# Summing the squares of the first norm on TensorE instead of on VectorE and GpSimd, in a two-layer encoder kernel

## The chip, the cores and the metric

One core of one Trainium2 chip runs the whole program. The metric is the device time of one execution in microseconds (us), the median of three runs. The engines are PE (TensorE: matmuls; PEld is its weight load), DVE (VectorE), ACT (ScalarE), POOL (GpSimd) and SP (SyncE, which issues the DMAs). Each engine works through its own queue in order.

## The reference

Two encoder layers over 512 tokens of 1024 features, float32. The change touches the start of layer 0, the first RMS norm:

```python
def rms(x, g):
    xf = x.astype(F32)
    y = xf * lax.rsqrt(jnp.mean(xf * xf, axis=-1, keepdims=True) + EPS)
    return (y * g.astype(F32)).astype(x.dtype)

    for layer in range(DEPTH):
        h = rms(x, g_mix[layer])
        (aq, ..., dv, gate) = jnp.split(h @ w_in[layer], split_points, axis=-1)
        o_a, o_b, o_c, o_d = ...                   # four attention branches
        br = jnp.einsum('bsmc,mcd->bsmd', o, w_branch[layer])
        g = jax.nn.sigmoid(gate.reshape(b, s, N_BRANCH, D_MODEL))
        x = x + jnp.einsum('bsmd,bsmd->bsd', g, br) @ w_out[layer]
        ...                                        # cross-attention, then the MLP
```

## The kernel before, in words

x lies transposed: 128 features on the partitions, the 512 tokens along the free axis, so 8 tiles `X` of 128x512 (`KD` = 8). Every large product is three fp32r matmuls (`mm3`, L177 to L179): high part by high part, high by low, low by high. So each weight tile is loaded (`wload`), cast to its high part `whi` by ACT (L299), and the low part `wlo` is subtracted by POOL in four pieces (L167 as called there). A norm's gain is multiplied into x ahead of the product (tiles `s`), and the per-token factor 1/rms (`r_mix`) is applied to the products, because it is known only later.

The start of layer 0 is `Norm.add_first`, once for each of the 8 tiles of x: it writes the scaled high part (ACT L348 or DVE L346) and low part (DVE L349), and ACT squares x (L355). The squares of even tiles are added up in the buffer `of` by DVE, those of odd tiles in the buffer `z` by POOL (L357). `Norm.finish` then sums both over the partitions: for each block of 128 tokens (`NTB` = 4) two fp32 matmuls with one column, the partial sum as weights and a column of ones as data (L364). DVE makes the mean (L367), POOL takes the power -1/2 (L368), DVE copies it to `r_mix` (L370). With `want_row=True` the same numbers are also wanted along the free axis: DVE spreads them on a diagonal (L374, which needs the identity matrix `idr`, loaded by DMA and cast at L234), PE multiplies that by ones (L377), and DVE copies the row to `Rrow` (L379).

Around it stand: `front_B0`, the first projection, four token blocks of 24 matmuls of 128x416 (banks `dn`, `dn`, `sc`, `sc`), each block read by ACT with `r_mix` (L412, L413), then reduced (L415), scaled (L669 to L675) and transposed by PE (L679); `layer_tables` (L269 to L289), small tables that DVE makes from one DMA each; `front_B` for pairs of heads (power on POOL at L716 to L718, scaling on DVE at L722 to L727); and `gate_piece`, which fills PE's time:

```python
        ps = psum("df")
        for k in range(KD):
            t = norm.xg[k]
            i = mm3(ps, gh[:, k, :], gl[:, k, :], t[:, 0, :], t[:, 1, :], k == 0, k == KD - 1)
            chain("fill", *i)
        z = tl("zg", [P, S])
        V.tensor_tensor(out=z, in0=ps, in1=norm.R, op=ALU.mult)
```

A gate piece is 24 matmuls of 128x512 into the bank `df`, of which there is one. Its reader is the multiplication with `Rrow` on DVE, L785, and the next gate piece can't start until it has run. `PB = dict(dn=2, sc=2, tr=2, pv=1, df=1)` gives the number of PSUM banks per name; of the SBUF buffers `of` and `z` there is one each, of `p` five.

What order an engine's instructions have is not written out: the tile scheduler of the framework merges the program's parts into a queue for each engine by its own estimates, and waits are on semaphores. An edit in one place can so shift rows on all engines.

Of the kernel before, what the change touches and what calls it, by code (L numbers as in the profile page):

```python
# [13 lines left out]
ALU = mybir.AluOpType  # L14
AX = mybir.AxisListType

P = 128
S = 512
D = 1024
KD = D // P  # L20
# [3 lines left out]
NTB = S // P  # L24
# [69 lines left out]
def kernel(  # L94
# [18 lines left out]
    V, A, G, T, SY = nc.vector, nc.scalar, nc.gpsimd, nc.tensor, nc.sync  # L113
# [12 lines left out]
    def tl(tag, shape, dt=F32):  # L126
        cnt[0] += 1
        return sp.tile(shape, dt, tag=tag, name=f"{tag}{cnt[0]}", bufs=BUFS[tag])

    def slot(dt=F32R, tag="s"):  # L130
        return tl(tag, [P, 2, S], dt)
# [4 lines left out]
    def ptile():  # L136
        return tl("p", [P, S + 2])

    def ztile():
        return tl("z", [P, S])  # L140

    def stat(n):
        return tl("st", [P, 8])[:, :n]
# [4 lines left out]
    def psum(tag, dt=F32):  # L148
        cnt[0] += 1
        return pp.tile([P, S], dt, tag=tag, name=f"{tag}{cnt[0]}", bufs=PB[tag])  # L150

    def const(name, shape, dt=F32):
        return cp.tile(shape, dt, tag=name, name=name)

    def f(ap):
        return ap.bitcast(F32)

    def bc(ap, axis, n):
        a = ap.unsqueeze(axis)
        shp = list(a.shape)  # L160
        shp[axis] = n
        return a.to_broadcast(shp)
# [28 lines left out]
    def big():  # L191

        rot["big"] += 1
        return ("dn", "dn", "df")[(rot["big"] - 1) % 3]
# [7 lines left out]
    ones = const("ones", [P, P])  # L202
# [21 lines left out]
    def fcol(l, name, i):  # L224
        o, _ = FEAT_OFF[name]
        return ftile[:, l, o + i:o + i + 1]
# [87 lines left out]
    class Norm:  # L314


        def __init__(self, l, gname):
            self.l, self.g = l, gname
            self.xg = [None] * KD
            self.ss = None  # L320
            self.r = self.R = self.R2 = None

        def add(self, m, x, c0=0):
# [17 lines left out]
        def add_first(self, m, x):  # L341

            g = fcol(self.l, self.g, m)
            t = self.xg[m] = slot()
            if m % 2:
                V.tensor_scalar(t[:, 0, :], x, g, None, op0=ALU.mult)  # L346
            else:
                A.activation(t[:, 0, :], x, AF.Copy, scale=g)  # L348
            V.scalar_tensor_tensor(out=t[:, 1, :], in0=x, scalar=g, in1=f(t[:, 0, :]), op0=ALU.mult, op1=ALU.subtract)  # L349
            if m < 2:  # L350
                q = tl("of", [P, S]) if m == 0 else tl("z", [P, S])
                self.ss = (self.ss or []) + [q]
            else:
                q = ptile()[:, :S]
            A.activation(q, x, AF.Square)  # L355
            if m >= 2:
                (G if m % 2 else V).tensor_tensor(out=self.ss[m % 2], in0=self.ss[m % 2], in1=q, op=ALU.add)  # L357

        def finish(self, want_row=False):
            ps = psum("tr")  # L360
            parts = self.ss if isinstance(self.ss, list) else [self.ss]
            for tb in range(NTB):
                for i, s in enumerate(parts):
                    T.matmul(ps[:, tb:tb + 1], lhsT=s[:, tb * P:(tb + 1) * P], rhs=ones[:, 0:1], start=i == 0,  # L364
                             stop=i == len(parts) - 1)
            r = stat(NTB)
            V.tensor_scalar(r, ps[:, :NTB], 1.0 / D, EPS, op0=ALU.mult, op1=ALU.add)  # L367
            G.tensor_tensor(out=r, in0=r, in1=mhalf[:, :NTB], op=ALU.pow)  # L368
            keep = rkeep[self.g]
            V.tensor_copy(keep, r)  # L370
            self.r = keep
            if want_row:
                dg = ztile()
                V.tensor_tensor(out=dg.rearrange("p (t c) -> p t c", t=NTB), in0=bc(idf, 1, NTB),  # L374
                                in1=bc(keep, 2, P), op=ALU.mult)
                pr = psum("tr")
                T.matmul(pr, lhsT=ones, rhs=dg, start=True, stop=True)  # L377
                self.R = Rrow
                V.tensor_copy(Rrow, pr)  # L379
# [624 lines left out]
    for l in range(L):  # L1004
# [39 lines left out]
        for spec in FILL.split("_"):  # L1044
            parts = []
# [9 lines left out]
        for i, (b, j) in enumerate(units):  # L1055
# [3 lines left out]
            parts = fill[i] if len(fill[i]) > 1 else [[]] + fill[i]  # L1059
# [35 lines left out]
        for i in range(4):  # L1095
            cs = slice(i * P, (i + 1) * P)
            ps = psum(big())
# [182 lines left out]
```

## Time and profile before

| what | value |
|---|---|
| runs | 2365.25, 2367.22, 2368.31 us; median 2367.22 |
| profiled execution | 2368.6 us, span of the profile 2366.8 us |
| busy share of the span | PE 97%, PEld 83%, DVE 59%, POOL 55%, ACT 49% |
| L357 (the additions) | 3 on DVE, 3 on POOL |
| granted TensorE clock | 0.993 of full speed on the mean |

Busy time alone says little here, since PE is busy nearly always: what counts is where PE waits, and who it waits for. The views used are the table of waits of one engine, the timeline (start, duration, engine, line, operation, out<-in, number of like instructions; in brackets the idle time ahead of it and what ended it), the summary of a source line, and the table of stretches. The distance from one start to the next is the time an instruction takes in a full queue, since neighbours overlap.

### The profile page before, as it was taken

The page shows a single profiled execution, that of the slowest core. Times are in us where ns is not written, and L with a number is a line of the kernel's source. Part 1 is how long each engine was busy: PE and PEld are TensorE (multiplying, and loading weights), DVE is VectorE, ACT ScalarE, POOL GpSimd, SP SyncE. Part 2 cuts the span into 40 slices and gives each one's busy share as a digit, 9 for nine tenths or more (in the row PEclk, how much of TensorE's full clock was granted, in tenths as well). Part 3 has the DMA queues.
Part 4 walks back from the last instruction along what each step waited for, and adds up shares of the span by engine and source line. Part 5 has one row for each costly group of instructions (what it writes and reads, how often), then busy time and mean ns, then how long its engine had stood idle before and what let it go on. Part 6 is the DMA issues. An engine that isn't in the chain of part 4 may idle for free.

```text
span 2366.8 us, 33717 instructions
## 1 busy us (share of the span) xinstructions
PE 2287.4 (97%) x12032; PEld 1962.2 (83%) x12032; DVE 1395.9 (59%) x2996; ACT 1153.7 (49%) x2269; POOL 1300.4 (55%) x1657
## 2 busy tenths in 40 slices
PE   7999999999999999999999999999999999999999
PEld 6788889887877788888888888898888778888887
DVE  7777676788964742222457676768888648222222
ACT  4555656655653642223345565566556446322321
POOL 7554454625365576666665535455452654766663
PEclk9999999999999999999999999999999999999999
DMA  5332242352454233333342213424425532323332
GB/s 174 96 98 68 84 142 79 122 162 73 152 184 144 76 98 96 91 98 98 106 134 92 87 56 106 133 79 154 128 88 169 168 109 84 107 91 97 98 95 84
DMA packets 90953, 260.36 MB, mean 110 GB/s; under 512 B 9832, under 2 KB 14568, under 8 KB 90784
## 3 DMA queue, kind: packets, MB, share of 16 engines
q1 hardware_dynamic: 90784, 258.20, 34.6%
q8 instruction: 95, 1.56, 0.3%
q14 instruction: 74, 0.61, 0.1%
HBM read 224.56 MB, written 33.60 MB: 109 GB/s over the span
## 4 chain that ended last, share of the span: by engine, by line
PE 72%; DVE 11%; POOL 5%; DMA 4%; issue 4%; ACT 3%; SPq 0%; POOLq 0%; ACTq 0%; DVEq 0%
PE dn L177 11%; PE dn L178 11%; PE dn L179 11%; PE df L177 8%; PE df L179 8%; PE df L178 8%; POOL wlo L167 4%; DMA wst<-in_wts_dram 3%; PE tr L476 2%; DVE pt L480 1%; ACT whi L299 1%; PE dn L403 1%; PE sc L177 1%; PE sc L179 1%; PE sc L178 1%
## 5 line engine op out<-in xcount | busy, mean ns | idle before, releaser
L167 POOL TENSOR_TENSOR wlo<-wst,whi 128x256 fp32r<-128x256 f32 (+3 forms) x1400 | 1073.9, 799 | 797.4 <-ACT whi L299 719.9
L299 ACT CAST whi<-wst 128x1024 fp32r<-128x1024 f32 (+3 forms) x350 | 349.8, 1002 | 660.1 <-PE dn L178 287.5
L177 PE MATMUL df<-s,whi 128*128 128x512 f32 (+1 forms) x967 | 383.7, 397 | 18.0 <-DVE zg L785 9.9
L179 PE MATMUL df<-s,wlo 128*128 128x512 f32 (+1 forms) x967 | 377.9, 391 | 0.0
L178 PE MATMUL df<-s,whi 128*128 128x512 f32 (+1 forms) x967 | 377.0, 390 | 0.0
L177 PE MATMUL dn<-whi,s 128*128 128x384 f32 (+4 forms) x736 | 248.2, 343 | 11.7 <-ACT s L348 7.6
L178 PE MATMUL dn<-wlo,s 128*128 128x384 f32 (+4 forms) x736 | 249.2, 341 | 1.1 <-POOL wlo L167 1.0
L179 PE MATMUL dn<-whi,s 128*128 128x384 f32 (+4 forms) x736 | 249.4, 340 | 0.0
L177 PEld LDWEIGHTS df<-s,whi 128*128 128x128 f32 x967 | 183.0, 189 | 56.8 <-DVE zg L785 13.7
L179 PEld LDWEIGHTS df<-s,wlo 128*128 128x128 f32 x967 | 183.1, 189 | 37.4 <-POOL wlo L167 0.7
L178 PEld LDWEIGHTS df<-s,whi 128*128 128x128 f32 x967 | 183.3, 190 | 33.2 <-issue 0.2
L177 PE MATMUL dn<-s,whi 128*128 128x512 f32 (+1 forms) x529 | 197.9, 377 | 3.1 <-ACT s L599 1.2
L178 PE MATMUL dn<-s,whi 128*128 128x512 f32 (+1 forms) x529 | 198.7, 377 | 0.4 <-DVE s L167 0.4
L179 PE MATMUL dn<-s,wlo 128*128 128x512 f32 (+1 forms) x529 | 198.0, 375 | 0.1
L177 PEld LDWEIGHTS dn<-whi,s 128*128 128x128 f32 x736 | 139.6, 191 | 21.0 <-ACT s L348 7.6
L479 ACT CAST pt<-tr 128x512 fp32r<-128x512 f32 (+1 forms) x224 | 123.0, 557 | 68.2 <-PE tr L476 66.7
L480 DVE TENSOR_TENSOR pt<-tr,pt 128x512 fp32r<-128x512 f32 (+1 forms) x224 | 142.7, 643 | 19.4 <-ACT pt L479 9.1
L178 PEld LDWEIGHTS dn<-wlo,s 128*128 128x128 f32 x736 | 140.0, 190 | 10.5 <-POOL wlo L167 3.8
L179 PEld LDWEIGHTS dn<-whi,s 128*128 128x128 f32 x736 | 139.8, 190 | 5.3
L311 POOL TENSOR_SCALAR sf<-sf 128x8 f32<-128x8 f32 (+2 forms) x44 | 13.5, 306 | 192.3 <-DVE sf L415 190.6
L177 PEld LDWEIGHTS dn<-s,whi 128*128 128x128 f32 x529 | 99.8, 190 | 21.8 <-ACT s L599 1.3
L178 PEld LDWEIGHTS dn<-s,whi 128*128 128x128 f32 x529 | 100.5, 190 | 19.0 <-DVE s L167 0.9
(392 smaller groups left out, 4895.4 us busy)
## 6 DMA issues: line engine op xcount, KB each, us to landing
wst<-in_wts_dram SPq DMA_DIRECT2D x272, 512.0 KB, 3.6
wst<-in_wts_dram SPq DMA_DIRECT2D x64, 384.0 KB, 3.0
yl<-yz SPq DMA_DIRECT2D x48, 512.0 KB, 3.6
yz<-zg SPq DMA_DIRECT2D x64, 256.0 KB, 2.1
yz<-yl SPq DMA_DIRECT2D x48, 256.0 KB, 3.0
bias<-tscr SPq DMA_DIRECT2D x16, 320.0 KB, 3.6
yl<-yz SPq DMA_DIRECT2D x16, 256.0 KB, 3.1
bias<-tscr SPq DMA_DIRECT2D x8, 448.0 KB, 3.7
```

The costliest lines, as they stand in the source:

```text
L167: (eng or V).tensor_tensor(out=dst, in0=src, in1=f(hi), op=ALU.subtract)
L177: a = T.matmul(ps, lhsT=lh, rhs=rh, start=first, stop=False)
L178: T.matmul(ps, lhsT=lh, rhs=rl, start=False, stop=False)
L179: b = T.matmul(ps, lhsT=ll, rhs=rh, start=False, stop=last)
L299: chain("wh", A.copy(hi[:, :n], st[:, :n]))
L311: G.tensor_scalar(dst, src, add, None, op0=ALU.add)
L403: T.transpose(ps[:rows_, i * P:(i + 1) * P], s, idn)
L476: T.transpose(ps[:, kb * P:(kb + 1) * P], src[:, kb * P:(kb + 1) * P], idn)
L479: A.copy(hi, pv)
L480: V.tensor_tensor(out=lo, in0=pv, in1=f(hi), op=ALU.subtract)
```

## The change

Each square goes into a buffer `p`, and right after it PE adds it to the sum: four matmuls of one column (one for each block of 128 tokens), accumulated over the 8 tiles in one bank `tr`. The additions are gone, and `finish` finds the sum ready. Later norms still use the sum in `of` (one matmul for each block, as before). Lines from L365 on have a number lower by one after the change; the new matmul is L356.

```diff
             else:
                 A.activation(t[:, 0, :], x, AF.Copy, scale=g)
             V.scalar_tensor_tensor(out=t[:, 1, :], in0=x, scalar=g, in1=f(t[:, 0, :]), op0=ALU.mult, op1=ALU.subtract)
-            if m < 2:
-                q = tl("of", [P, S]) if m == 0 else tl("z", [P, S])
-                self.ss = (self.ss or []) + [q]
-            else:
-                q = ptile()[:, :S]
+            if m == 0:
+                self.ps = psum("tr")
+            q = ptile()[:, :S]
             A.activation(q, x, AF.Square)
-            if m >= 2:
-                (G if m % 2 else V).tensor_tensor(out=self.ss[m % 2], in0=self.ss[m % 2], in1=q, op=ALU.add)
+
+            for tb in range(NTB):
+                T.matmul(self.ps[:, tb:tb + 1], lhsT=q[:, tb * P:(tb + 1) * P], rhs=ones[:, 0:1], start=m == 0 and tb == 0,
+                         stop=m == KD - 1 and tb == NTB - 1)
 
         def finish(self, want_row=False):
-            ps = psum("tr")
-            parts = self.ss if isinstance(self.ss, list) else [self.ss]
-            for tb in range(NTB):
-                for i, s in enumerate(parts):
-                    T.matmul(ps[:, tb:tb + 1], lhsT=s[:, tb * P:(tb + 1) * P], rhs=ones[:, 0:1], start=i == 0,
-                             stop=i == len(parts) - 1)
+            ps = self.ps
+            if ps is None:
+                ps = psum("tr")
+                for tb in range(NTB):
+                    T.matmul(ps[:, tb:tb + 1], lhsT=self.ss[:, tb * P:(tb + 1) * P], rhs=ones[:, 0:1], start=True, stop=True)
```

The queues change in the mixer of layer 0 (PE to about row 3250 of 10786, DVE to about row 550 of 2832) and are the same behind it. Three places show how.

**PE, first projection.** Names: `dn_283`/`dn_301`, `sc_347`/`sc_365` are banks of the projection before/after, `df_251` is the first gate piece, `tr_203`/`tr_152` the bank of the sum, `tr_218`/`tr_236` that of the row. Before, the last seven rows of the sum stood behind 76 matmuls of the projection and the gate piece, and the matmul of the row had only five matmuls of the projection behind it:

```order
L178 MATMUL sc_347<-wlo_142,s_183 128x416
L364 MATMUL tr_203<-ones,z_157 128x1
L364 MATMUL tr_203<-ones,of_152 128x1
...
L179 MATMUL df_251<-s_149,wlo_245 128x512
...
L177 MATMUL sc_379<-whi_141,s_183 128x416
L377 MATMUL tr_218<-z_216,ones 128x512
L178 MATMUL sc_379<-wlo_142,s_183 128x416
```

After:

```order
L179 MATMUL dn_333<-whi_108,s_149 128x416
L356 MATMUL tr_152<-ones,p_180 128x1 x4
L356 MATMUL tr_152<-ones,p_189 128x1 x4
L356 MATMUL tr_152<-ones,p_198 128x1 x4
L356 MATMUL tr_152<-ones,p_207 128x1 x4
L356 MATMUL tr_152<-ones,p_216 128x1 x4
L178 MATMUL dn_301<-wlo_120,s_168 128x416
...
L178 MATMUL dn_333<-wlo_120,s_177 128x416
L376 MATMUL tr_236<-z_234,ones 128x512
L179 MATMUL dn_333<-whi_119,s_177 128x416
```

Now 39 matmuls of the projection and all 32 of the sum stand ahead of the row's, and 57 of the projection behind it; the first gate piece has left the projection and follows it.

**DVE, from the tables to the row.** `st_212`/`st_230` is the mean, `z_216`/`z_234` the diagonal. Before:

```order
L280 TENSOR_TENSOR p_231<-bias_222 128x128
L367 TENSOR_SCALAR st_212<-tr_203 128x4
L282 TENSOR_REDUCE st_233<-p_231 128x2
L370 COPY r_mix<-st_212 128x4
L234 CAST idr<-z_195 128x128
L284 TENSOR_TENSOR nlam<-st_233 128x1
L285 TENSOR_SCALAR nlam<-nlam 128x1
L415 TENSOR_REDUCE sf_309<-dn_283 128x1 x3
L234 CAST jr<-z_198 128x128
...
L374 TENSOR_TENSOR z_216<-idr,r_mix 128x512
```

After:

```order
L280 TENSOR_TENSOR p_249<-bias_240 128x128
L234 CAST jr<-z_225 128x128
L366 TENSOR_SCALAR st_230<-tr_152 128x4
L282 TENSOR_REDUCE st_251<-p_249 128x2
L369 COPY r_mix<-st_230 128x4
L373 TENSOR_TENSOR z_234<-idr,r_mix 128x512
```

Both casts of identities now stand ahead of the mean (that of `idr` further up), and the diagonal follows `r_mix` at once. The tables still stand ahead of the mean.

**DVE, two gate pieces later.** `df_995`/`df_1013` is the same gate piece before and after, `tok_551`/`tok_569` the same pair of heads, `sf_552`/`sf_570` its factors. Before:

```order
L415 TENSOR_REDUCE sf_552<-dn_559 128x2
L167 TENSOR_TENSOR spl_589<-tok_517,spl_589 128x4x32
L785 TENSOR_TENSOR zg_1020<-df_995,Rrow 128x512
L174 COPY T_505<-dn_605 96x2x256
L722 TENSOR_TENSOR tok_551<-tok_551,sf_552 128x2x256
```

After:

```order
L174 COPY T_523<-dn_623 96x2x256
L721 TENSOR_TENSOR tok_569<-tok_569,sf_570 128x2x256
L722 TENSOR_TENSOR tok_569<-tok_569,sf_570 128x2x64
L174 COPY T_524<-dn_635 96x2x256
L724 TENSOR_TENSOR tok_569<-tok_569,gbn 128x2x64 x2
L726 TENSOR_TENSOR tok_569<-tok_569,gqr 128x64 x2
L167 TENSOR_TENSOR spl_655<-tok_569,spl_655 128x4x64
L784 TENSOR_TENSOR zg_1038<-df_1013,Rrow 128x512
```

The reader of the `df` bank has moved from ahead of the scaling of the heads to behind it. On POOL the four subtractions of one weight tile (128x160 each) now stand between the small power's first two steps and the power itself (L715, L716 and L717 after).

## Rows read from the trace of the kernel before

**Rows 1.** The page, parts 1 and 5: busy time and share of the span by engine, and one of the costliest groups (busy time, mean ns of one | idle time ahead of it).

```profile
PE 2287.4 (97%) x12032; PEld 1962.2 (83%) x12032; DVE 1395.9 (59%) x2996; ACT 1153.7 (49%) x2269; POOL 1300.4 (55%) x1657
...
L480 DVE TENSOR_TENSOR pt<-tr,pt 128x512 fp32r<-128x512 f32 (+1 forms) x224 | 142.7, 643 | 19.4 <-ACT pt L479 9.1
```

**Rows 2.** Waits of PE in the first 45 us: what it waited for, us in total, times, longest.

```profile
PE dn L177 <- ACT s L348: 7.6, 1, 7.6
PE df L177 <- ACT whi L299: 2.2, 1, 2.2
PE dn L679 <- DVE tok L673: 1.6, 1, 1.6
PE tr L364 <- DVE of L357: 0.7, 1, 0.7
```

**Rows 3.** Timeline of DVE, from the last table to the diagonal.

```profile
28.04 0.28 DVE L280 TENSOR_TENSOR p<-bias 128x128 f32<-128x128 f32 x1
28.24 0.15 DVE L367 TENSOR_SCALAR st<-tr 128x4 f32<-128x4 f32 x1
...
29.52 0.17 DVE L370 COPY r_mix<-st 128x4 f32<-128x4 f32 x1 [0.88 <-POOL st L368]
31.90 0.23 DVE L234 CAST idr<-z 128x128 fp32r<-128x128 f32 x1 [2.21 <-DMA z<-in_ident_dram]
...
34.25 0.68 DVE L374 TENSOR_TENSOR z<-idr,r_mix 128x512 f32<-128x512 f32 x1
```

**Rows 4.** Timeline of PE, the end of the sum before (each one-column matmul is two records): the first pair of seven in a row, and the matmul that follows them.

```profile
25.76 0.28 PE L364 MATMUL tr<-ones,z 128*128 128x1 f32 x2
...
27.24 0.48 PE L179 MATMUL df<-s,wlo 128*128 128x512 f32 x1
```

**Rows 5.** Line L357, the additions: durations in ns (least, median, longest), first and last start in us.

```profile
L357 DVE TENSOR_TENSOR of<-of,p x3: 1123/1124/1784, 10.1 to 18.6; 128x512 f32<-128x512 f32 x3
L357 POOL TENSOR_TENSOR z<-z,p x3: 1293/1723/1749, 13.5 to 23.8; 128x512 f32<-128x512 f32 x3
```

**Rows 6.** Timeline of PE at its start: two neighbours at the first pace, two at the later one.

```profile
11.28 0.55 PE L179 MATMUL dn<-whi,s 128*128 128x416 f32 x1
11.62 0.55 PE L177 MATMUL dn<-whi,s 128*128 128x416 f32 x1
...
13.10 0.35 PE L178 MATMUL dn<-wlo,s 128*128 128x416 f32 x1
13.29 0.35 PE L179 MATMUL dn<-whi,s 128*128 128x416 f32 x1
```

**Rows 7.** Timeline of PE, from the row's matmul to the second gate piece.

```profile
35.55 1.02 PE L377 MATMUL tr<-z,ones 128*128 128x512 f32 x2
36.01 0.75 PE L178 MATMUL sc<-wlo,s 128*128 128x416 f32 x1
...
42.18 0.47 PE L177 MATMUL df<-s,whi 128*128 128x512 f32 x1 [2.22 <-ACT whi L299]
42.49 0.40 PE L178 MATMUL df<-s,whi 128*128 128x512 f32 x1
42.72 0.40 PE L179 MATMUL df<-s,wlo 128*128 128x512 f32 x1
```

**Rows 8.** Timeline of DVE from 71 to 79 us: the reader of a gate piece and the scaling of a pair of heads.

```profile
71.66 0.68 DVE L785 TENSOR_TENSOR zg<-df,Rrow 128x512 f32<-128x512 f32 x1
72.26 0.68 DVE L174 CAST T<-dn 96x512 fp32r<-96x512 f32 x1
74.57 1.22 DVE L722 TENSOR_TENSOR tok<-tok,sf 128x512 f32<-128x512 f32 x1 [1.64 <-POOL sf L718]
...
77.95 0.47 DVE L727 TENSOR_TENSOR tok<-tok,gqr 128x64 f32<-128x64 f32 x2
```

**Rows 9.** Timeline of PE: waits at the start of gate pieces and around them, in layer 0.

```profile
72.40 0.50 PE L177 MATMUL df<-s,whi 128*128 128x512 f32 x1
...
79.85 0.67 PE L403 MATMUL dn<-idr,spl 128*96 128x128 f32 x4 [1.11 <-ACT spl L732]
80.72 0.54 PE L177 MATMUL df<-s,whi 128*128 128x512 f32 x1 [0.20 <-DVE zg L785]
...
169.52 0.49 PE L177 MATMUL df<-s,whi 128*128 128x512 f32 x1 [1.17 <-DVE zg L785]
...
257.84 0.50 PE L177 MATMUL df<-s,whi 128*128 128x512 f32 x1 [0.97 <-DVE zg L785]
...
280.62 0.63 PE L476 MATMUL tr<-idr,p 128*128 128x128 f32 x4 [1.26 <-DVE p L505]
```

**Rows 10.** Timeline of POOL at the same place: two of four subtractions of 128x160, then the steps of the power for a pair of heads.

```profile
68.94 1.20 POOL L167 TENSOR_TENSOR wlo<-wst,whi 128x160 fp32r<-128x160 f32 x2
71.50 0.35 POOL L716 TENSOR_SCALAR sf<-sf 128x8 f32<-128x8 f32 x1 [1.36 <-DVE sf L415]
...
72.24 2.30 POOL L718 TENSOR_TENSOR sf<-sf,mhalf 128x12 f32<-128x12 f32 x1
```

**Rows 11.** Table of stretches: us, busy time and instructions of PE, PEld, DVE, ACT, POOL, then the granted clock of PE (1.00 is full), the DMA share and GB/s.

```profile
42.20:47.00 4.80, 4.80 (x14) 3.81 (x15) 4.61 (x17) 2.17 (x8) 3.65 (x5) 0.64 0.77 183
81.00:84.50 3.50, 3.50 (x10) 2.68 (x10) 0.53 (x2) 0.59 (x2) 3.05 (x4) 0.51 0.23 80
169.50:284.00 114.50, 111.93 (x669) 100.53 (x670) 83.08 (x196) 67.60 (x150) 46.40 (x67) 1.00 0.25 80
```

More of the change, by code (lines that the diff above doesn't have):

```diff
@@ L319, in __init__ @@
             self.xg = [None] * KD
-            self.ss = None
+            self.ss = self.ps = None
             self.r = self.R = self.R2 = None
```

## The prediction

> **What bounds the kernel now.** I began with the busy shares: PE works 97% of the span, DVE, the next, 59% [rows 1]. So the time is PE's own work, plus PE's waits, plus what PE does at half clock. An engine other than PE counts only where PE waits for it. The second view is therefore PE's waits in the first 45 us, where the sum of squares is made: 7.6 us until x is there, 0.7 us for an addition of L357, 1.6 us for a product of L673, 2.2 us for the weights of the second gate piece [rows 2]. Only the 0.7 us is named after the code that goes. The third view is the way from the sum to the row: the mean runs on DVE at 28.24, but right behind the last table, L280 at 28.04 [rows 3], though the matmuls of the sum had ended by 27.24 [rows 4]. It stood in DVE's queue, not in wait for PE. That is what the edit can move: DVE's queue in front of the mean is shortened by three additions.
>
> The order of all queues changes with it, up to a third of PE's rows. So I went through both orders and gave every row its duration from the trace; the terms below are the places where PE's wait comes out different by over 1 us.
>
> **Removed.** Three additions on DVE, 1.12 + 1.78 + 1.12 = 4.02 us, and three on POOL, 1.75 + 1.72 + 1.29 = 4.76 us [rows 5]. Neither is on PE; what they free is worked out in the next part but one.
>
> **Added on PE.** 32 one-column matmuls in place of 8, so 24 more. Seven in a row took 25.76 to 27.24, 0.211 us each [rows 4], about as much as a matmul of 416 columns (0.19 at the later pace [rows 6]). Together 24 x 0.211 = 5.1 us; at the first pace (0.34 against 0.19 for the same 416 columns [rows 6]) it would be up to 9. The bounds are 0, if PE would stand there anyway, and +5.1 to +9 if not. I take 0, for this reason: ahead of the row's matmul the new order has 39 matmuls of the projection and the 32. 39 x 0.19 + 32 x 0.211 = 14.2 us, and some 15 of them at the first pace add 15 x 0.15 = 2.3. From 7.6 us [rows 2] PE is through by 24.1 at the latest (the squares are made before it, and the first eight of the new matmuls stand ahead of everything, so they run while PE waited before). The row's data comes later, as follows.
>
> **The row is earlier for DVE, and PE stands in front of it.** DVE's mean: 28.24 - 4.02 + two casts of 0.23 that moved ahead of it (L234 [rows 3]) = 24.7. From mean to the end of `r_mix` 29.52 + 0.17 - 28.24 = 1.45, then the diagonal at once, 0.68 [rows 3]: 26.8. PE, ready at 24.1 or before, waits 2.7 us or more for a diagonal that before was ready while PE was still in the projection. Behind it stand: the row's matmul 0.46 (35.55 to 36.01 [rows 7]), 57 of the projection x 0.19 = 10.7, the first gate piece 24 x 0.23 = 5.5 (42.49 to 42.72 [rows 7]), and two groups of transposes, some 0.7 each. 26.8 + 0.5 + 10.7 + 5.5 + 1.4 = 44.9 for the start of the second gate piece, which was at 42.18 [rows 7]: **+2.7 us**. The old waits of 1.6 and 2.2 us are inside this: they are gone, and cover nothing. The identity's DMA, which came late before (DVE waited 2.21 us [rows 3]), no longer needs the buffer `z` of the sum and is issued early; I cost it at nothing, and if it were late again the row would wait for it, not the mean.
>
> **The bank `df`, two pieces later.** Before, the reader of the bank ran at 71.66, ahead of the scaling of the heads, and PE's next piece started at 72.40 almost without a wait [rows 8, 9]. Now it stands behind the scaling, which needs POOL's power, and on POOL four subtractions of 0.6 (half of the 1.20 for two [rows 10]) have moved in front of that power. POOL: 71.50 to 72.24 = 0.74, + 2.4, + 2.30 [rows 10] = 5.4. DVE from there: 74.57 to 78.42 = 3.85 for the scaling, 0.6 for the copy to `T`, about 0.3 for the split, 0.68 for the reader itself [rows 8]: 5.4. Together 10.8 us after POOL begins. In the meantime PE has one gate piece (5.5) and 16 transposes (0.6 each eight), 6.9 at most with gaps. So PE waits about 3.7 us. Against it stand the waits of 1.11 and 0.20 that follow in the trace [rows 9], which this covers only in part: **+3.5 us** with the small waits before it.
>
> **Two more readers of `df` moved behind other work.** Of the gate piece `df_1493` in the new order (the third after the one above) the reader now stands behind work for attention and for a further pair of heads. From the moment when PE ends the piece that is one evacuation (0.64, the mean of L480 [rows 1]), a reduction of as many columns, taken as the same, four small rows that I estimate at 1.0 together from the 0.47 for two of L727 [rows 8], and the reader's own 0.68: 3.0 us, against eight transposes on PE, 0.9 to 1.1 us: **+1.9**. For the piece at 257.84, which waits 0.97 already [rows 9], the scaling again comes first and POOL's power starts later, behind two subtractions of 0.6: I put that wait at 3.2, so **+2.2**.
>
> **Given back.** PE comes 6 to 8 us later into the rest of layer 0 while DVE's queue there is as long as before, so waits for DVE shrink: 1.17 at 169.52 to some 0.5, 1.26 at 280.62 to some 0.4 [rows 9], and a few of 0.3 to 0.5; **-2.8** in all.
>
> Sum: 2.7 + 3.5 + 1.9 + 2.2 - 2.8 = **+7.5 us**. The profiled execution took 2368.6 (span 2366.8), so 2376.1; it lies 1.4 above the median of the runs, 2367.2, and the same sum on the median gives **2374.7**. The terms have errors of 1 to 2 us each, mostly where a queue's order decides; from these alone I give 2371.5 to 2378.
>
> [...]
>
> **Rivals.**
> 1. *No change that can be measured* (within 0.2%, 4.7 us, about what a measurement of this kernel can tell from no change). The front goes as above, but the `df` readers don't decide: DVE's wait for POOL's power is shorter, because POOL has 4.76 us less to do and its subtractions run earlier, and PE, late by 2.7, finds the bank free. Then 2.7, half of the 7.6 of the three places, and -2.8 are about +3.7: 2370.9. For it: POOL is busy 55% [rows 1]; against it: the power itself is 2.30 us and now stands behind the subtractions.
> 2. *Faster.* The row's diagonal is there when PE comes: DVE's tables run through earlier, and PE never stands. Then the waits of 0.7, 1.6 and 2.2 go, 5.1 of new work comes, and the first eight of the new matmuls lie in PE's first wait (8 x 0.34 = 2.7 at the first pace): the second gate piece starts at 42.18 - 4.5 + 5.1 - 2.7 = 40.1, so -2.1, and if the `df` readers also keep up, with the -2.8 given back, -4.9: 2362.3. It decides at the mean: it would have to run before about 21 instead of 24.7, but the tables, whose last runs at 28.04 before [rows 3], still stand in front. Little speaks for it.
> 3. *More than forecast.* Each new wait of over 2.5 us (at the row, at the two `df` pieces) is followed by a stretch at half clock, as in the trace behind 1.6 + 2.2 [rows 11]: three of 1.7, less the one that goes: +3.4 on the forecast, 2378.1. [...]
>
> **How the numbers follow.** Forecast 0.60, rival 1 0.18, rival 2 0.05, rival 3 0.17. The forecast's own lower end reaches into the band of no change with about 0.02. So faster 0.05, same 0.20, slower 0.75. The range takes the forecast, nearly all of rival 3 (to 2380.5) and the upper half of rival 1: 2369 to 2380.5.
>
> **What would show it.** Right: the L356 matmuls end before 24, PE waits 2 us or more at L376, whose diagonal ends near 26.8; the second gate piece starts near 45; the piece that was at 72.40 starts near 79 after a wait of 3 to 4 us for L784; from 400 us on everything is later by a constant 6 to 9 us. Wrong: if PE waits for L356's squares or the first projection runs longer at half clock (then the 5.1 is on the path); if the gate pieces start without waits for L784 (rival 1); if L376 doesn't wait (rival 2); if the clock is low in stretches behind the new waits (rival 3).

## The result and the profile after

The change makes the kernel slower: 2382.39 us in the median of 6 runs (2376.46 to 2390.01) against 2366.65 for the kernel before on the same chip, a ratio of 1.0072 with a 95% interval of 1.0057 to 1.0087, or +17 us (13 to 21; the medians lie 15.7 apart). A second measurement beside other kernels gave 1.0070 (1.0057 to 1.0084). The forecast was +7.5, with 2380.5 as its upper end: the sign was right, the size was not.

The profiled execution is the longest of the six (2390.0, span 2388.2), so some of its numbers are above the median's; a second trace, of the same kernel in another run (e5, span 2375.3, the shortest of its six), stands beside it where that matters.

The page's busy times, against [rows 1]: PE has 20 us more, as has its weight load; DVE and POOL have 9.1 and 4.4 less, ACT 2.0 more.

```profile
PE 2307.4 (97%) x12080; PEld 1981.7 (83%) x12080; DVE 1386.8 (58%) x2993; ACT 1155.7 (48%) x2269; POOL 1296.0 (54%) x1654
```

**The front.** The waits of PE in the first 60 us, which answer to [rows 2]:

```profile
PE tr L356 <- ACT p L353: 5.5, 2, 4.5
PE df L177 <- DVE kr_raw L586: 1.8, 1, 1.8
```

The waits of 0.7, 1.6 and 2.2 us are gone, and PE starts at 4.5 instead of 7.6, as expected. A wait of 1.8 at the second gate piece is new: the first gate piece now runs right ahead of it, and L784, the reader of their bank, starts on DVE only at 50.50. But there is no wait at L376, where the forecast had 2.7 us or more. PE's timeline shows why; these rows answer to [rows 4, 6, 7]:

```profile
4.52 1.86 PE L356 MATMUL tr<-ones,p 128*128 128x1 f32 x8 [4.52 <-ACT p L353]
7.41 1.87 PE L356 MATMUL tr<-ones,p 128*128 128x1 f32 x8 [1.03 <-ACT p L353]
...
12.06 1.70 PE L356 MATMUL tr<-ones,p 128*128 128x1 f32 x8
...
15.85 8.53 PE L356 MATMUL tr<-ones,p 128*128 128x1 f32 x40
...
27.50 0.55 PE L178 MATMUL dn<-wlo,s 128*128 128x416 f32 x1
27.85 0.55 PE L179 MATMUL dn<-whi,s 128*128 128x416 f32 x1
...
29.02 0.36 PE L178 MATMUL dn<-wlo,s 128*128 128x416 f32 x1
29.22 0.35 PE L179 MATMUL dn<-whi,s 128*128 128x416 f32 x1
...
30.92 1.02 PE L376 MATMUL tr<-z,ones 128*128 128x512 f32 x2
...
51.33 0.47 PE L177 MATMUL df<-s,whi 128*128 128x512 f32 x1 [1.75 <-DVE kr_raw L586]
```

Twenty one-column matmuls in a row (40 records) took 15.85 to 24.23, 0.42 us each, twice the 0.211 of [rows 4]. The 416-column matmuls start 0.35 apart until 28.2 and 0.19 apart behind that. So PE runs at the lower of the two paces until 28.2; before the change the same pace ended at 12.8 ([rows 6] stand on both sides of it). The row's matmul starts at 30.92 because PE gets to it then: its diagonal was ready at 26.6, which the rows of DVE show (they answer to [rows 3]):

```profile
20.94 0.28 DVE L280 TENSOR_TENSOR p<-bias 128x128 f32<-128x128 f32 x1
...
24.41 0.16 DVE L366 TENSOR_SCALAR st<-tr 128x4 f32<-128x4 f32 x1 [3.05 <-PE tr L356]
...
25.69 0.17 DVE L369 COPY r_mix<-st 128x4 f32<-128x4 f32 x1 [0.93 <-POOL st L367]
25.90 0.69 DVE L373 TENSOR_TENSOR z<-idr,r_mix 128x512 f32<-128x512 f32 x1
```

The forecast's 24.7 for the mean and 26.8 for the diagonal came out, at 24.41 and 26.59, but not for its reason: DVE was through with the tables and the cast by 21.4 and then waited 3.05 us for the sum.

**The gate pieces.** Their waits, from PE's timeline (answering to [rows 9]; the pieces that started at 72.40, 103.69 and 257.84 before):

```profile
84.45 0.50 PE L177 MATMUL df<-s,whi 128*128 128x512 f32 x1 [1.39 <-DVE zg L784]
...
122.36 0.50 PE L177 MATMUL df<-s,whi 128*128 128x512 f32 x1 [2.31 <-DVE zg L784]
...
269.84 0.50 PE L177 MATMUL df<-s,whi 128*128 128x512 f32 x1 [2.42 <-DVE zg L784]
```

**The clock later.** In the table of stretches (columns as in [rows 11]) five stretches of layer 0 lie at half clock behind the front, where the kernel before had two; the second and third of the five are right behind the second and third of these waits:

```profile
76.10:79.50 3.40, 3.40 (x9) 2.62 (x8) 0.42 (x1) 0.02 (x1) 2.95 (x3) 0.50 0.71 200
...
123.90:127.30 3.40, 3.40 (x10) 2.66 (x9) 1.33 (x7) 0.30 (x1) 3.15 (x5) 0.50 0.64 184
270.70:274.10 3.40, 3.40 (x13) 2.62 (x11) 0.69 (x3) 0.55 (x1) 2.25 (x4) 0.50 0.50 183
315.00:318.40 3.40, 3.40 (x12) 3.40 (x11) 3.06 (x7) 1.25 (x3) 2.53 (x5) 0.51 0.82 249
352.60:356.00 3.40, 3.40 (x10) 2.62 (x9) 1.09 (x3) 1.36 (x2) 1.36 (x3) 0.50 0.73 220
```

Three of the five are there in the second trace too:

```profile
120.10:123.50 3.40, 3.40 (x10) 2.64 (x9) 2.49 (x8) 0.88 (x3) 2.55 (x5) 0.50 0.50 174
266.90:270.30 3.40, 3.40 (x9) 2.63 (x9) 1.28 (x4) 1.06 (x2) 2.25 (x4) 0.50 0.61 193
311.30:314.70 3.40, 3.40 (x13) 3.21 (x12) 2.93 (x8) 1.33 (x3) 2.97 (x5) 0.50 0.90 273
```

**The account.** All kernels of this study run the same matmuls, apart from those of the sum, up to the gate piece that starts at 459.8 us before the change. So its start can be split into PE's waits, the time of the sum's matmuls (start to start), 418.5 us (the other matmuls, each at the median pace of its kind in the trace of before) and what they took above that. Of this last, half clock is 6 of 17.1 us before, 13 of 22.8 in the change and under 1 of 12.6 in e10, worked out from the rows at the lower level; the remainder is 10 to 14 in every kernel. I worked the table out from PE's timeline, one trace for each kernel:

| kernel | start of the piece | PE's waits | sum's matmuls | above 418.5 | all runs: ratio to before, interval |
|---|---|---|---|---|---|
| before | 459.8 | 22.5 | 1.7 | 17.1 | 1 |
| the change | 477.9 | 23.0 | 13.5 | 22.8 | 1.0072 (1.0057 to 1.0087) |
| the change, again (e5) | 473.0 | 21.1 | 13.5 | 19.9 | 1.0070 (1.0057 to 1.0084) |
| 128 columns (e1) | 464.8 | 21.8 | 8.6 | 15.9 | 1.0033 (1.0021 to 1.0045) |
| 64 columns (e8) | 469.9 | 23.7 | 9.5 | 18.2 | 1.0040 (1.0028 to 1.0052) |
| additions gone only (e2) | 466.3 | 24.8 | 3.6 | 19.4 | 1.0038 (1.0025 to 1.0050) |
| matmuls added only (e3) | 474.1 | 26.2 | 7.5 | 21.9 | 1.0058 (1.0045 to 1.0072) |
| ones as weights (e4) | 468.9 | 21.7 | 6.9 | 21.9 | 1.0026 (1.0017 to 1.0035) |
| two tiles (e6) | 454.2 | 17.8 | 2.7 | 15.2 | 0.9976 (0.9967 to 0.9985) |
| three tiles (e7) | 460.7 | 23.1 | 3.5 | 15.6 | 1.0016 (1.0007 to 1.0025) |
| gate piece held (e9) | 461.7 | 16.6 | 11.5 | 15.1 | 1.0030 (1.0020 to 1.0039) |
| held, 128 columns (e10) | 456.6 | 16.8 | 8.7 | 12.6 | 0.9995 (0.9986 to 1.0004) |
| held, ones as weights (e11) | 460.8 | 18.4 | 6.9 | 17.1 | 1.0007 (0.9998 to 1.0016) |
| held, the same reduced (e12) | 455.7 | 19.0 | 4.0 | 14.3 | 0.9998 (0.9988 to 1.0008) |
| held, 128 columns reduced (e13) | 455.7 | 18.8 | 4.8 | 13.6 | 0.9983 (0.9974 to 0.9992) |

Behind that piece the traces differ by single stretches at half clock (six behind it before, seven in the change), and such stretches come and go between runs of one kernel, as those at 76 and 352 us do between the change's two traces; so the ratios of all runs decide and the account says where to look. A difference of 1 or 2 us in one trace is not to be leaned on. In the change against before the table reads: waits +0.5 (-1.4 in the second trace), the sum's matmuls +11.8, the rest +5.7 (+2.8).

### The profile page after: what moved, and what is told of

It reads as the page before. It is cut to its first block, busy times and chain, and to the rows that moved or that the text cites. A ratio compares the mean times of both kernels' runs of the same rounds, so it can differ in the third digit from the quotient of the medians.

```text
span 2388.2 us, 33802 instructions
## 1 busy us (share of the span) xinstructions
PE 2307.4 (97%) x12080; PEld 1981.7 (83%) x12080; DVE 1386.8 (58%) x2993; ACT 1155.7 (48%) x2269; POOL 1296.0 (54%) x1654
## 4 chain that ended last, share of the span: by engine, by line
PE 75%; DVE 11%; POOL 5%; issue 4%; DMA 3%; ACT 2%; SPq 0%; POOLq 0%; ACTq 0%; DVEq 0%
PE dn L177 12%; PE dn L178 12%; PE dn L179 12%; PE df L177 9%; PE df L178 9%; PE df L179 8%; POOL wlo L167 3%; PE tr L475 2%; DMA wst<-in_wts_dram 2%; PE dn L402 1%; PE sc L177 1%; PE sc L178 1%; PE sc L179 1%; DVE pt L479 1%; POOL sf L312 1%
## 5 line engine op out<-in xcount | busy, mean ns | idle before, releaser
L177 PE MATMUL dn<-whi,s 128*128 128x384 f32 (+4 forms) x736 | 250.6, 346 | 4.2 <-DVE sf L414 4.0
L179 PE MATMUL dn<-whi,s 128*128 128x384 f32 (+4 forms) x736 | 252.2, 343 | 0.0
L479 DVE TENSOR_TENSOR pt<-tr,pt 128x512 fp32r<-128x512 f32 (+1 forms) x224 | 143.1, 644 | 28.5 <-ACT pt L478 14.3
L177 PEld LDWEIGHTS dn<-whi,s 128*128 128x128 f32 x736 | 141.0, 193 | 13.6 <-DVE sf L414 5.3
L177 PEld LDWEIGHTS dn<-s,whi 128*128 128x128 f32 x529 | 99.3, 189 | 21.1 <-ACT s L598 1.3
```

What stands on the lines that cost most here:

```text
L177: a = T.matmul(ps, lhsT=lh, rhs=rh, start=first, stop=False)
L179: b = T.matmul(ps, lhsT=ll, rhs=rh, start=False, stop=last)
L479: V.tensor_tensor(out=lo, in0=pv, in1=f(hi), op=ALU.subtract)
```

## The experiments

The theories: A, the 32 matmuls are on PE's path and run, with much of the projection, at half clock; B, the forecast's: the loss is waits from the new order of the queues; C, which joined after the first four runs: both, with a price for each.

### e1: 128 columns instead of one

```diff
-                T.matmul(self.ps[:, tb:tb + 1], lhsT=q[:, tb * P:(tb + 1) * P], rhs=ones[:, 0:1], ...
+                T.matmul(self.ps[:, tb * P:(tb + 1) * P], lhsT=q[:, tb * P:(tb + 1) * P], rhs=ones, ...
 ...
```

> As the change, but each of the 32 matmuls of the sum has 128 columns of ones as data instead of one (a block of 128 equal columns in the bank; the mean reads one of each). Queues as in the change but for 23 of 10790 rows of PE, near the sum. Theory A (the 32 matmuls are on PE's path, at half clock, and PE stays at half clock because one-column matmuls are most of what it does): the clock rises by 15 us instead of 28, a matmul of the sum takes 0.21 to 0.24 us instead of 0.43, the row's matmul starts near 26 instead of 30.9, and the time is 5 to 9 us below the change, 2373 to 2377. If only their number counts and not what they stream: the time of the change, 2382, clock up near 28. Theory B (the waits that the new queue order brings are the loss, as forecast): order the same, so 2380 to 2384.

Measured: 1.0033 against the 1.0072 and 1.0070 of the change, so 9 us less, for 128 times the columns. The summary of line L356 in the change, and then in this kernel (durations in ns: least, median, longest):

```profile
L356 PEld LDWEIGHTS tr<-ones,p x64: 285/333/333, 4.5 to 24.0; 128*128 128x128 f32 x64
L356 PE MATMUL tr<-ones,p x64: 205/352/373, 4.5 to 24.0; 128*128 128x1 f32 x64
```

```profile
L356 PEld LDWEIGHTS tr<-ones,p x64: 188/192/337, 4.7 to 18.0; 128*128 128x128 f32 x64
L356 PE MATMUL tr<-ones,p x64: 270/275/582, 4.7 to 18.1; 128*128 128x128 f32 x64
```

A weight load takes 192 ns instead of 333, and the sum is through at 18 instead of 24 us. The pace was up at 8.5 us, the row's matmul came at 24.57. A holds for half the loss. What is left, +8, is not half clock in the front; e10 below shows what it is.

### e2: the additions taken away, and nothing else

```diff
-            if m >= 2:
-                (G if m % 2 else V).tensor_tensor(out=self.ss[m % 2], in0=self.ss[m % 2], in1=q, op=ALU.add)
```

> The kernel before without the six additions; the squares of tiles 2 to 7 are made and not summed (the norm leaves out six of eight tiles), so 8 one-column matmuls as before, which can now run first. Theory A: no added matmuls, so no loss: 2360 to 2369, the second gate piece at 40 to 44 us. Theory B (an earlier row moves the readers of the gate pieces behind other work): 2371 to 2378, with waits of 2 us and more for L784's counterpart.

Measured: 1.0038, +9 us, though nothing was added (six of the eight tiles are left out of the sum): A misses, B's range holds. The largest entry of PE's waits until the piece of the account:

```profile
PE df L177 <- DVE zg L783: 5.7, 6, 2.3
```

The second gate piece starts at 40.2, 2 us earlier than before, and the gain is lost again behind it. The order is one of its own here, with the first gate piece behind the projection. The order of the queues alone can cost more than the additions.

### e3: the matmuls added, the additions kept

```diff
             if m >= 2:
+                if m == 2:
+                    self.ps = psum("tr")
+                for tb in range(NTB):
+                    T.matmul(self.ps[:, tb:tb + 1], lhsT=q[:, tb * P:(tb + 1) * P], rhs=ones[:, 0:1], ...)
```

> The kernel before with its six additions, plus 24 one-column matmuls of the squares of tiles 2 to 7 into a bank that nobody reads. Theory A: the matmuls alone make the loss: +8 to +14 over before (2375 to 2381), the clock rises later than 12.8 us. Theory B: the row comes no earlier, so the order of the gate pieces' readers stays near that of before: at most +5 (24 x 0.21 us), 2367 to 2372.

Measured: 1.0058, +13.7 us, as A said. But it doesn't speak against B: PE's order is that of the change (of its first 3000 records, those of the sum left out, 22 differ from the change and 889 from before), though the row comes no earlier. The reason given for B, the early row, falls with it; e4, whose row's matmul stands behind 93 of the 96 of the projection, has the new order too. A's clock missed: the pace rose at 11.2, not later than 12.8, and fell again. The twenty matmuls in a row ran from 13.50 to 18.02, 0.226 us each, and from 18.0 to 24.8 the granted clock was 0.50.

### e4: ones as weights, squares as data

```diff
-            for tb in range(NTB):
-                T.matmul(self.ps[:, tb:tb + 1], lhsT=q[:, tb * P:(tb + 1) * P], rhs=ones[:, 0:1], ...)
+            T.matmul(self.ps, lhsT=ones, rhs=q, start=m == 0, stop=m == KD - 1)
 ...
+            if self.ps is not None:
+                ss, one = tl("of", [P, S]), 1
+                V.tensor_copy(ss[:1, :], self.ps[:1, :])
```

> The squares are summed over partitions the other way round: ones as weights (128x128), the square as data, 8 matmuls of 512 columns, so the sums lie along the free axis; DVE copies one row of them, and four one-column matmuls of one partition turn them to one per token. PE work for it: 8 x 0.46 + 4 x 0.2 = 4.5 us against 13.7 in the change. Theory A: clock up near 13 us, time 2364 to 2372, below the change by 10 or more. Theory B: the queue order changes as much as in the change, so 2370 to 2378.

Measured: 1.0026, +6 us, 10 below the change, where the two theories' ranges overlap, so the time alone doesn't decide: the pace rose at 9.4, the sum's matmuls took 6.9 us, and the order was that of the change.

### e5: the change again

> The change itself once more, beside the three kernels below on one chip and with a second trace. Theory A+C (A: the 32 matmuls cost 13.5 us of PE at half clock in place of 1.7; C: the new queue order costs some 6 to 8 more, as waits for readers of gate pieces and as stretches at half clock): +14 to +18 over before, clock up near 28 us, the stretches at half clock near 270, 315 and 352 us again. If those stretches are chance, they lie elsewhere.

Measured: 1.0070. The pace was up at 28.0, and the stretches at 120, 267 and 311 came again; those at 76 and 352 did not. At nearly the same places of the program e1, e3, e4 and e8 have the first two of these three, all but e8 the third, and e3, e4 and e8 the one at 352. So the three mostly come with this order, and the others come and go.

### e6 and e7: two tiles and three tiles

In the sum's loop: `for tb in range(NTB if m in (0, 7) else 0)` and `(0, 3, 7)`. The scheduler gives e6 the order of before and e7 that of the change.

> The change with the matmuls of tiles 0 and 7 alone: 8 one-column matmuls, no additions, the norm leaves out six of eight tiles. Behind the front (44 of 10771 rows of PE) its queues are those of the kernel before, not those of the change. Theory A+C: no added matmuls and the old order, so no loss: -4 to +2 against before (2360 to 2366 where before is 2364). If taking the additions away is itself what hurts (run without additions: +9), it is +6 to +10 here too.

> As the run with two tiles, with tile 3 as well: 12 one-column matmuls, no additions, five tiles left out. Four matmuls more (0.9 to 1.7 us), but the queues behind the front are now those of the change (109 of 10775 rows differ) instead of those before. Theory A+C: the order alone costs 6 to 8, so +6 to +9 against before, and 5 to 9 below the change (20 matmuls of 0.43 less). If order costs nothing: +0 to +3.

Measured: 0.9976 and 1.0016, -5.7 and +3.8 us: e6 lies 2 us below its range and e7 2 us below the range for theory A+C, but the difference between them fits. Four one-column matmuls, 0.8 us in the account, and the other order make 9 us between them. PE's waits to the piece of the account, first e6, then e7:

```profile
PE df L177 <- DVE zg L784: 4.3, 7, 1.0
...
PE dn L402 <- ACT spl L731: 1.1, 1, 1.1
```

```profile
PE df L177 <- DVE zg L784: 7.6, 7, 2.3
PE tr L356 <- ACT p L353: 4.6, 1, 4.6
PE dn L402 <- ACT spl L731: 4.0, 2, 3.4
```

It is the places that the forecast named: readers of the `df` bank, and what PE transposes for the pairs of heads. And e6 shows what taking the additions away is worth in the old order: -5.7 us.

e7 also shows that such a wait need not bring half clock. The two long waits of the change are there, and the clock behind them stayed at full; PE's timeline, then the table of stretches:

```profile
111.91 0.50 PE L177 MATMUL df<-s,whi 128*128 128x512 f32 x1 [2.32 <-DVE zg L784]
...
257.82 0.49 PE L177 MATMUL df<-s,whi 128*128 128x512 f32 x1 [2.33 <-DVE zg L784]
```

```profile
112.00:115.40 3.40, 3.40 (x15) 2.81 (x16) 2.79 (x10) 1.58 (x4) 3.15 (x6) 1.00 0.52 181
258.00:261.40 3.40, 3.40 (x20) 2.77 (x20) 2.04 (x5) 1.19 (x2) 2.13 (x4) 1.00 0.57 193
```

### e8: 64 columns

The edit of e1 with 64 columns (`rhs=ones[:, 0:64]`).

> The change with 64 columns of ones in place of one; the 20 matmuls of tiles 3 to 7 still stand in a row, and 81 of 10790 rows of PE differ. If it is the columns that bring the clock up (not the interleaving that the run with 128 columns also had): clock up by 20 us, 0.21 to 0.3 us for a matmul of the sum, +7 to +11 over before. If it was the interleaving: as the change, +14 to +18.

Measured: 1.0040, +9.5; pace up at 13.5, with the twenty matmuls still in a row. So the other matmuls that e1 had between them are not needed for the early rise; with one column and the same order it came at 28.

### e9: the change, with the first gate piece held in its old place

```diff
-                mm3(ps[:, :width], ...)
+                i = mm3(ps[:, :width], ...)
+                if norm is first and width == 416 and tb == 3 and k == 2:
+                    tc.add_manual_dep(i[0].ins, tails["fill"].name,
+                                      mybir.DependencyInfo(mybir.DependencyClass.NoSync, ...), reason="gate0")
 ...
```

> The change with one thing added: an ordering without a semaphore, by which the fourth block of the first projection (its third k) comes after the first gate piece in PE's queue, as it did before the change. All 32 one-column matmuls stay, 20 of them in a row. From the second gate piece on the queues are nearly those of the kernel before (199 of 10771 rows of PE differ, all but some in the front). Theory A+C: the order alone cost 6 to 8, so 2370 to 2374 where before is 2364 and the change 2380; clock still up only near 28 us. If the order costs nothing: 2378 to 2382.

Measured: 1.0030, 9 us below the change with the same work. This is what the order was: the change had pushed the first gate piece out of the projection, where it had been a filler (71 of the 96 matmuls of the projection stand ahead of it before, all 96 after, 78 here; it starts at 24.73, 43.10 and 37.61), and so every gate piece of the following stretch came one place later against the attention's work. Of the 11.3 us between e5 and e9 in the account, 4.5 are waits, 2.0 the sum's matmuls, 4.8 the rest; but the trace of e9 is of the fastest of its nine runs (2364.3, their median 2369.4), so the price of the order, 9 us, is taken from the ratios. The table of stretches for 260 to 360 us, in the change and then here:

```profile
260.00:360.00 100.00, 94.15 (x527) 84.66 (x526) 66.00 (x153) 55.17 (x121) 51.03 (x73) 0.95 0.36 112
```

```profile
260.00:360.00 100.00, 96.92 (x556) 87.88 (x557) 68.54 (x160) 56.01 (x123) 46.53 (x68) 1.00 0.38 125
```

In this trace the half clock there is gone too. Over all traces, from 26 us to the piece of the account, the kernels with the new order have two to five stretches at half clock (the change 5, e5 3, e1 3, e8 4, e3 5, e4 5, e7 2), those with the old order none to two (before 2, e6 and e11 1, the four others with the hold none). One point of the expectation missed: the clock was up at 12.0, not near 28. It then fell again:

```profile
12.00:15.40 3.40, 3.40 (x28) 3.39 (x27) 3.36 (x5) 2.87 (x5) 3.40 (x5) 1.00 1.01 386
15.40:25.70 10.30, 10.30 (x41) 10.08 (x41) 7.20 (x22) 0.00 (x0) 6.22 (x8) 0.50 0.25 98
25.70:30.00 4.30, 4.30 (x21) 3.77 (x21) 2.02 (x10) 1.08 (x2) 0.85 (x1) 1.00 0.00 0
```

At half clock from 15.4 to 25.7, with PE busy in every moment of it; the one-column matmuls in a row ran from 13.86 to 20.94. (Ahead of a trace's first clock record the table says 1.00 too: in the change from 24.2 to 28.2, where the 416-column matmuls start 0.35 apart, as they do here from 21.3 to 25.5 at 0.50. There only the pace tells.)

### e10 to e13: both causes taken away, and cheaper sums

e10 is e1 with e9's hold, e11 is e4 with it, and e12 and e13 are e11 and e10 with squares and ones in reduced float32: `q = tl("p", [P, S + 2], F32R)[:, :S]` and a copy `onesr` of the ones.

> Both causes taken away at once: 128 columns of ones (clock up early) and the first gate piece held in its old place. Theory A+C: the run with 128 columns alone was +8.8, less 6 to 8 for the order: +0 to +3 against before. If the two are one cause, +6 to +9.

> Ones as weights, 8 matmuls of 512 columns (two records each, 0.46 us), one row turned back by four small matmuls, with the first gate piece held in its old place. Theory A+C: the run without the hold was +6.2, less 6 to 8: -2 to +1 against before, a correct sum without additions that costs nothing. If the two are one cause: +5 to +7.

> As the run before it, with squares and ones rounded to the reduced float32 of the other matmuls, so that each of the 8 is one record instead of two: about 8 x 0.23 = 1.8 us less PE work. Theory A+C: -4 to 0 against before, up to 2 below the run with full float32.

> As the run with 128 columns and the gate piece held, but squares and ones rounded to the reduced float32 of the other matmuls, so each of the 32 is one record instead of two. Theory A+C: what keeps that run 5 us above the one with two tiles is PE's time for the sum (8.7 us against 2.7), so half of it goes, 4 us: -3 to -6 against before, the first correct sum without additions that gains. If the rest has another cause: -2 to +1.

Measured: 0.9995, 1.0007, 0.9998 and 0.9983, or -1.2, +1.7, -0.5 and -4.0 us; e10 and e11 miss their ranges by about 1 us, less than their intervals. The two causes add up: 128 columns take 9 us off the change and 8 off e9, the hold takes 9 off both the change and e1. e10, without both, is level with before; it has 8.7 us of the sum's matmuls where before has 1.7, and 5.7 us less of waits. e13 halves the records to one for each matmul, the account goes from 8.7 to 4.8, and the kernel is 4 us faster than before (2 to 6): so PE's own time for the sum was what was left. It is the one version with the whole sum that beats both kernels.

## Why the prediction was wrong

**The step that failed is "I take 0" for the added matmuls.** It rested on "some 15 of them at the first pace": I took over from the trace of before that the clock rises at 12.8, though what was to be done until then had changed. With 32 one-column matmuls among the first 71, the pace stayed at the lower one until 28.2 in the change, all 32 cost double (13.5 us in the account instead of 6.8), and PE, forecast to be through at 24.1, came to the row at 30.92. So it was PE, not the diagonal, that was late. Up to the second gate piece the sum's matmuls are +11.8 in the account, and only PE's waits, which shrank from 12.1 to 7.3, stand against them. The prediction named this among its signs of being wrong, but gave it no chance of its own. At the second gate piece it made +9.1 (42.18 to 51.33) instead of +2.7, and +8.6 at the one behind it, after the half clock that before had from 43.5 on (0.51 from 43.50 to 47.00).

**The waits behind the second gate piece were right in sum, in part by luck.** Behind the second gate piece I had 3.5 + 1.9 + 2.2 - 2.8 = +4.8. In the account, the change's waits from there to 460 us are 15.7 (15.3 in the second trace) against 10.4 before: +5.3 and +4.9. Single terms were off and made up for each other: 1.39 instead of 3.7 at the first place (where the working, 10.8 less 6.9, gives 3.9), since POOL's power had ended at 79.05, before PE was through with the piece in front, and the bank's reader then stood behind a copy of PE's own transposes; 2.31 against 1.9 forecast at the second; 2.42 against 3.2 at the third; the waits of 1.17 at 169.52 and 1.26 at 280.62 went to nothing. Over the whole stretch to 460 us the waits hardly changed (+0.5, -1.4). Runs e6, e7 and e9 show that these waits come from the order, not from the matmuls. The reason that theory B gave for the order, an earlier row, was not tested by itself, and e3 and e4 show the same order without it.

**Half clock had no term in the forecast's sum** and should have had one: it was rival 3. The 1.7 us that rival 3 has for a stretch is an estimate from [rows 11] (4.80 us at 0.64); no run shows what one stretch costs. What the runs showed: behind the front five stretches of 3.4 us at 0.50 or 0.51 in the change, three in its second trace and two before, and in the account 13 us of half clock, the front's included, against 6. The rest above 418.5 grew by 5.7 and 2.8, nearly all of it behind the front (two gate pieces after the row it is 5.1 in the change and 5.6 before). Rival 3 has such a stretch behind each long wait. The trace of the change has it behind 122.36 (wait 2.31, 0.50 from 123.9) and 269.84 (2.42, 0.50 from 270.7), and in e9 both the waits and these stretches are gone (no wait for a gate piece's reader over 1.0, the clock 1.00 from 60 to 360). The trace of e7 does not agree: the clock stayed at 1.00 behind the same two waits (2.32 and 2.33). In front of the stretch at 315 there are only three waits of 0.4 to 0.7. So half clock came more often with this order, and what decides in the single case stays open. I had costed the order at its waits alone, +4.8; e9 against the change prices it, with its clock, at 9 us.

So the loss, worked out from the ratios: the additions and their waits are worth -6 (e6), 24 more matmuls, mostly at the lower pace, +13 (e9 less e6), the order +9 (the change less e9): +16 to +17. They add up to the whole because each step starts where the one before ends, so the sum proves nothing by itself, and e9 differs from e6 in some rows of the front besides the matmuls. Each of the three has an uncertainty of 2 to 4 us. The forecast had +7.5 as the sum of a front at +2.7 and waits at +4.8.

What stays open: why the scheduler pushes the first gate piece out with 12 one-column matmuls in e7 and not with 8 in e6; in e2 it does so with 8. Its estimates leave no trace on the chip; that it does is read from the queues.

## What to carry to other kernels

The pace that I read early in the trace of before went with the work done then: with 32 one-column matmuls among it, the time at which the pace rises went from 12.8 to 28.2 us. So where an edit puts many short matmuls early, make the cost of PE's work at both paces (here 0.211 and 0.42 us for a one-column matmul) before it is called covered. Where a scheduler orders the queues, hold a filler in its place by an ordering without a semaphore and measure the edit with and without it: here the same edit was +17 or +7.

## What the hardware showed that I had not expected

- In the change PE worked without a wait from 9.14 us on, and the pace rose only at 28.2, behind the twenty one-column matmuls of 15.85 to 24.2; in e9 the clock fell while PE was busy without a gap, full from 12.0 to 15.4 and 0.50 behind, as one-column matmuls ran. With 64 or 128 columns in place of one the pace was up at 13.5 and 8.5 us instead of 28.
- A float32 matmul of 128 weights with 128 columns took about as long as one with a single column at the same pace. At the upper pace, four with 128 columns took 10.00 to 10.81 in e1, 0.20 us each, against 0.211 for seven in a row with one [rows 4]; at the lower, the first eight of e1 took 4.69 to 8.37, 0.46 each, against 0.42.
- One of DVE's tables took 0.28 us with POOL at rest and 1.40 with POOL at work. In the change POOL's subtractions end at 20.06, and L273, right at that time, took 0.28 us (L271 ahead of it 0.66, as before the change):

```profile
19.48 0.66 DVE L271 SCALAR_TENSOR_TENSOR gbn<-bias 128x64 f32<-128x64 f32 x1
20.06 0.28 DVE L273 SCALAR_TENSOR_TENSOR gx<-bias 128x128 f32<-128x128 f32 x1
```

Before the change L273 took 1.40 us, at 23.88, with POOL at its third addition. That POOL is the cause was not tried by itself.
